# Sliding-window scores with 64-row matmuls against each group's own keys, in a two-layer hybrid decoder trunk

## The chip, the cores and the metric

The kernel runs on one NeuronCore of a Trainium2 chip, as one program. The metric is the device time of one execution in microseconds (us). The core has five engines that run side by side, each with its own queue of instructions in order: TensorE (matrix multiplies; the profile lists its multiplies as PE and its weight loads as PEld), VectorE (DVE), ScalarE (ACT), GpSimd (POOL) and SyncE (SP, which here issues most DMAs). They wait for one another through semaphores. Matmuls read from SBUF, the on-chip memory of 128 partitions, and write to PSUM, the accumulators, which are divided into banks of 512 fp32 values per partition.

## What is computed

The reference is a trunk of two layers over 256 tokens of width 1024. Each layer has a half-step SwiGLU, a layer norm, three token mixers side by side on the same normalised stream (gated DeltaNet, sliding-window attention with sinks, attention over a memory), gates that merge them, an output projection, a layer norm, and a second half-step SwiGLU with a layer norm. The change touches the sliding-window attention alone:

```python
SWA_HEADS = 8; SWA_KV_HEADS = 2; SWA_DH = 64; WINDOW = 128; SEQ = 256

def sliding_window_attention(q, k, v, sinks):
    Hkv, G, dh, W = SWA_KV_HEADS, SWA_HEADS // SWA_KV_HEADS, SWA_DH, WINDOW
    nb = S_ // W
    qb = q.reshape(B_, nb, W, Hkv, G, dh)
    kb, vb = band(k), band(v)          # the block before and the block itself
    s = jnp.einsum('bnqhgd,bnkhd->bnhgqk', qb, kb) * (dh ** -0.5)
    s = jnp.where(mask, s, NEG_INF)    # 0 <= t - key < W
    m = jnp.maximum(s.max(-1, keepdims=True), sink)
    p = jnp.exp(s - m)
    p = p / (p.sum(-1, keepdims=True) + jnp.exp(sink - m))
    o = jnp.einsum('bnhgqk,bnkhd->bnqhgd', p, vb)
```

Eight query heads of 64 features share two groups of keys and values, four heads each. The 256 tokens make two blocks of 128; the first block sees 128 keys, its own, the second sees 256.

## The kernel before

**Numbers.** Most products are made from pairs: an fp32 value is split into a high part in the type fp32r and a low part, also fp32r, that holds what the high part leaves over (`split`, line 115: a ScalarE cast, then a VectorE subtraction). A product is three matmuls, high by high, high by low and low by high (`mm3`, line 131). A matmul in fp32r is one record in the trace, one in plain fp32 is two.

**Weights.** All weights come as one stream, in units of 128 partitions by 1024 columns (`unit`, line 99): a DMA on SP's queue into `raw`, the cast to `whi` on ScalarE, the subtraction to `wlo` on VectorE. The consumers take them in stream order.

**Order.** Inside `mixers` (line 460) the order of TensorE's work is fixed by hand: every matmul and transpose goes through `pe` (line 121), which keeps program order while `pinned` is set. Steps of the sliding attention, the memory attention and the DeltaNet recurrence are placed between groups of projection matmuls by `weave` (line 137): a generator yields after each group, and the functions listed under that number run next. On the other engines instructions keep the order in which a scheduler places them.

**Sliding attention.** The projection of the keys is one bank with 128 features by 256 tokens: features 0 to 63 belong to key group 0, features 64 to 127 to group 1 (line 760). Lines 761 to 763 split it into `swk`, a high and a low tile of 128 partitions by 2 groups by 256 tokens. In slot `v` only the 64 partitions of group `v` are written; the other 64 were set to zero once, at the start of the program, by two ScalarE copies (lines 92 to 94). The queries (`sq_`, line 660) are laid out so that one tile of 128 partitions holds a head of group 0 in its upper half and a head of group 1 in its lower half. `sq_` index `2 * hh + j` picks such a pair.

`w_scores(tb, hh)` (line 665) makes the scores of token block `tb` for the four heads of `hh`. One `mm3` per pair takes the 128x128 query tile as weights and moves both slots of the zero-padded keys, 2 x `nk` columns, where `nk` is 128 at `tb` 0 and 256 at `tb` 1: the zeros keep the groups apart. At `tb` 0 both pairs fit into one PSUM bank, at `tb` 1 each takes a bank of its own. The banks come from `at()` (line 65), a pool of two that the transposes and values of both attentions share. A VectorE instruction (line 677) scales each bank, adds the mask and writes `pp`. The softmax follows: the row maximum, the sinks, exponentials on ScalarE, the reciprocal, the scaling (lines 678 to 692). `w_turn` transposes the probabilities, `w_values` multiplies them with the values.

In the order of work (lines 939 to 958) `w_scores(0, 0)` and `w_scores(0, 1)` stand after steps 7 and 8 of the first gates projection, `w_scores(1, 0)` after step 4 of the first branch projection, `w_scores(1, 1)` after step 2 of the second gates projection. `w_values(0)` comes one step after `w_scores(1, 0)`. All of it happens once in each layer.

Of the kernel before, what the change touches and what calls it, by code (L numbers as in the profile page):

```python
# [11 lines left out]
F32R = mybir.dt.float32r  # L12
I32 = mybir.dt.int32
AF = mybir.ActivationFunctionType
ALU = mybir.AluOpType
AX = mybir.AxisListType

P = 128
D = 1024
S = 256  # L20
# [18 lines left out]
def tile_trunk(ctx, tc, x, xT, mem, wst, lnp, memln, cvw, rows, cst, out):  # L39
    nc = tc.nc  # L40
    pc = ctx.enter_context(tc.tile_pool(name="pc", bufs=1))
# [16 lines left out]
    def T(pool, shape, tag, dt=F32, bufs=None):  # L58
        kw = {} if bufs is None else {"bufs": bufs}
        return pool.tile(shape, dt, tag=tag, name=nm(tag), **kw)  # L60
# [4 lines left out]
    def at():  # L65
        return T(psT, [P, 512], "at")
# [22 lines left out]
    nea = pc.tile([P, NL, 4], F32, name="nea")  # L89
    zero = pc.tile([P, 1], F32, name="zero")  # L90
    nc.gpsimd.memset(zero, 0.0)
    swk = [pc.tile([P, 2, S], F32R, name=f"swk{i}") for i in range(2)]
    for t in swk:
        nc.scalar.copy(t.rearrange("p v k -> p (v k)"), zero.to_broadcast([P, 2 * S]))


    pos = [0]
# [17 lines left out]
    def split(hi, lo, src):  # L115
        nc.scalar.copy(hi, src)  # L116
        return nc.vector.tensor_tensor(lo, src, hi.bitcast(F32), op=ALU.subtract).ins  # L117
# [3 lines left out]
    def pe(ins):  # L121

        return tc.keep_in_program_order(ins) if pinned[0] else ins

    def matmul(*a, **k):
        return pe(nc.tensor.matmul(*a, **k))  # L126
# [4 lines left out]
    def mm3(o, l, r, first, last, skip=False):  # L131
        (lh, ll), (rh, rl) = l, r
        matmul(o, lh, rh, start=first, stop=False, skip_group_check=skip)
        matmul(o, lh, rl, start=False, stop=False, skip_group_check=skip)
        matmul(o, ll, rh, start=False, stop=last, skip_group_check=skip)

    def weave(work, steps):

        for n, _ in enumerate(work, 1):
            for f in steps.get(n, ()):  # L140
                f()

    def projB(xt, nt, kpu, behind=None):
        g = projB_parts(xt, nt, kpu, behind)
        while True:
            try:
                next(g)
            except StopIteration as e:
                return e.value
# [37 lines left out]
    def halves(xt, use):  # L187

        for i in range(2):
            (b,) = yield from projB_parts(xt, 2, 4)  # L190
            use(i, b)
# [256 lines left out]
    def memory_kv(mT, behind):  # L448
        mx = (lambda k: mT[k // 4][:, k % 4, :], lambda k: mT[2 + k // 4][:, k % 4, :])
        mkT = (T(pu, [P, 4, S], "u10", F32R), T(pu, [P, 4, S], "u7", F32R))  # L450
        for i, b in enumerate(projB(mx, 4, 2)):
            split(*(t[:, 2 * i:2 * i + 2, :] for t in mkT), b)
        mv_ = T(pu, [P, 2, 512], "u11")
        outs = [[acc()] for _ in range(2)]
        projA(mx, 512, 2, KD, outs, behind=behind, held=range(4))
        for tb in range(2):
            nc.scalar.copy(mv_[:, tb, :], outs[tb][0])
        return mkT, mv_

    def mixers(l, hT, mkT, mv_, post):  # L460
# [8 lines left out]
        for tb in range(2):  # L469
            a, b = outs[tb]  # L470
# [70 lines left out]
        def col(tag):  # L541
            return T(pu, sh, tag)
# [11 lines left out]
        t = col("spt")  # L554
# [105 lines left out]
        sq_ = (T(pu, [P, 4, S], "u5", F32R), T(pu, [P, 4, S], "sql", F32R))  # L660
# [4 lines left out]
        def w_scores(tb, hh):  # L665

            ts = slice(tb * P, (tb + 1) * P)
            nk = P if tb == 0 else 2 * P
            msk = cs[:, C_SW + P:C_SW + 2 * P] if tb == 0 else cs[:, C_SW:C_SW + 2 * P]
            pr = wpr[tb, hh] = T(p2, [P, 4, S], "pp")  # L670
            for j in range(0, 2, 2 * P // nk):

                nj = 2 * P // nk
                ps = at().rearrange("p (j v k) -> p j v k", j=nj, v=2)
                for i in range(nj):
                    mm3(ps[:, i], [t[:, 2 * hh + j + i, ts] for t in sq_], [t[:, :, 0:nk] for t in swk], True, True)
                nc.vector.scalar_tensor_tensor(pr[:, 2 * j:2 * j + 2 * nj, :nk], ps.rearrange("p j v k -> p (j v) k"), 0.125, msk.unsqueeze(1).to_broadcast([P, 2 * nj, nk]), op0=ALU.mult, op1=ALU.add)
            mxs = T(p3, [P, 2, 2], "mx")
            sums = T(p3, [P, 4], "sums")
            sk = T(p3, [P, 2, 2], "sk")  # L680
            sink = sinks[:, 2 * hh:2 * hh + 2, :]
            flat = lambda t: t.rearrange("p i v -> p (i v)")
            nc.vector.tensor_reduce(flat(mxs), pr[:, :, :nk], axis=AX.X, op=ALU.max)
            nc.vector.tensor_tensor(mxs, mxs, sink, op=ALU.max)
            nc.vector.tensor_tensor(sk, sink, mxs, op=ALU.subtract)
            nc.scalar.activation(flat(sk), flat(sk), AF.Exp)
            nc.vector.tensor_scalar(flat(mxs), flat(mxs), -1.0, None, ALU.mult)
            for h in range(4):
                nc.scalar.activation(pr[:, h, :nk], pr[:, h, :nk], AF.Exp, bias=mxs[:, h // 2, h % 2:h % 2 + 1], accum_out=sums[:, h:h + 1])
            nc.vector.tensor_tensor(sums, sums, flat(sk), op=ALU.add)  # L690
            wpr["end"] = nc.vector.reciprocal(sums, sums).ins
            [nc.scalar.mul(pr[:, h, :nk], pr[:, h, :nk], sums[:, h:h + 1]) for h in range(4)]
# [65 lines left out]

        weave(halves(xt, use_xq), {3: [tok_v]})
        (b,) = projB(xt, 1, 8)  # L760
        for kv in range(2):
            hs = slice(kv * 64, kv * 64 + 64)
            split(swk[0][hs, kv, :], swk[1][hs, kv, :], b[hs, 0, :])
        weave(halves(xt, use_sq), {
            1: [decay],
            2: [lambda: spread(0), lambda: x_scores(0)],
# [153 lines left out]
        def branch(n, o):  # L920
# [22 lines left out]
            5: [lambda: x_turn(1)],  # L943
            6: [lambda: x_values(1)],
            7: [lambda: w_scores(0, 0)],
            8: [lambda: w_scores(0, 1)]})
        weave(branch(0, oX), {
            2: [lambda: w_turn(0, 0)],
            3: [lambda: w_turn(0, 1), begin_inverse],
            4: [lambda: w_scores(1, 0)]})  # L950
        weave(gates(1), {
            1: [lambda: w_values(0), double],
# [59 lines left out]
    for l in range(NL):  # L1012
        mT = []
        mid = memory_T(mT, l)
        if l == 0:
            mid.update({5: small, 7: lambda: xres(0), 9: lambda: xres(1)})
        post = Post(lnp[l, 0, 0], lnp[l, 0, 1])
        f1.rest(hT, 4, [((pu, "u12"), (pu, "u13")), ((p2, "gt"), (p2, "gt"))], post, mid, ends)
        kv = memory_kv(mT, post.end)
        if l == 0:  # L1020
            nc.scalar.activation(nea, rw[:, :, 8:12], AF.Exp)
            nc.vector.tensor_scalar(nea, nea, -1.0, None, ALU.mult)
        post2 = Post(lnp[l, 1, 0], lnp[l, 1, 1])
        mixers(l, post.hT, *kv, post2)
        f2 = Ffn()
        begin(f2, post2.hT)
        last = l == NL - 1
        post = Post(lnp[l, 2, 0], lnp[l, 2, 1], last)
        f2.rest(post2.hT, 6, [((pu, a), (pu, b)) for a, b in (("w0", "w1"), ("w2", "w3"), ("u11", "u12"))] + [((pu, "u13"), (p2, "pp"))], post, behind=post2.end)
        ends = post.end  # L1030
        if not last:
            f1, hT = Ffn(), post.hT
            begin(f1, hT)
# [86 lines left out]
```

## Time and profile before

| | |
|---|---|
| median of 3 runs | 1296.47 us (1295.87 to 1298.31) |
| profiled execution, its own time | 1298.02 us |
| its span, first to last instruction | 1296.2 us |
| mean granted TensorE clock | 0.998 |
| instructions | 20444 |
| DMA | 240.25 MB, mean 185 GB/s |

The profile is of one execution. Its views: a summary of busy times by engine; groups of instructions by line, engine, operation, tiles and shape, with their count; one tile's instructions; a timeline, in which neighbouring equal instructions are merged into a row with a count; windows, with the busy time of each engine in a stretch; and the chain of work that ended last, followed back from the last instruction to whatever released each step. A timeline row gives the start, the length of the merged stretch, the engine, the line, the operation, output and inputs by tile name, the rows and columns of the array that are used (128\*128), the shape that is moved, the count, and in brackets the idle time before it with what ended it. Lines 126 and 129 are helpers through which all matmuls and transposes of the mixers go, so the tile names tell them apart: `at<-swk,u` and `at<-swk,sql` are the scores with the high and the low part of the queries. Matmuls are pipelined: each record lasts longer than the step to the next one.

### The profile page before, as it was taken

How to read it: one execution, taken by the hardware profiler on the slowest of the kernel's cores; microseconds unless marked ns; L12 is line 12 of the kernel's file. 1: busy time of each engine (PE TensorE's matmuls, PEld its weight loads, DVE VectorE, ACT ScalarE, POOL GpSimd, SP SyncE). 2: the span in 40 equal slices, each digit the busy share in tenths (PEclk: the TensorE clock that was granted, in tenths of full speed). 3: DMA queues.
4: the chain of work that ended last, by engine and by line, in shares of the span. 5: the costliest groups of instructions: out<-in, count | busy, mean ns of one | idle time of the engine just before them, and what ended most of it. 6: DMA issues, size and time to landing. Idle time of an engine off the chain costs nothing.

```text
span 1296.2 us, 20444 instructions
## 1 busy us (share of the span) xinstructions
PE 1277.9 (99%) x7832; PEld 1116.2 (86%) x7832; DVE 888.4 (69%) x1430; ACT 708.5 (55%) x1177; POOL 77.2 (6%) x135
## 2 busy tenths in 40 slices
PE   8999999999999999999999999999999999999997
PEld 6888889999878888888888888899988788888886
DVE  6787556796647777665677674759867388777645
ACT  6656444666674546554455654456656654565541
POOL 0000000102311000000000000000033100000000
PEclk9999999999999999999999999999999999999999
DMA  7867564654533636555665555556453256455553
GB/s 266 276 210 244 193 229 128 220 174 135 161 131 130 228 129 211 191 185 192 228 222 200 188 186 192 199 175 201 163 165 131 98 182 224 149 194 194 189 189 111
DMA packets 68577, 240.25 MB, mean 185 GB/s; under 512 B 8160, under 2 KB 9312, under 8 KB 68480
## 3 DMA queue, kind: packets, MB, share of 16 engines
q1 hardware_dynamic: 66176, 232.53, 53.1%
q0 software_dynamic: 2304, 6.43, 1.8%
q8 instruction: 61, 1.00, 0.3%
q14 instruction: 36, 0.29, 0.1%
HBM read 235.64 MB, written 3.28 MB: 184 GB/s over the span
## 4 chain that ended last, share of the span: by engine, by line
PE 89%; DVE 4%; DMA 4%; ACT 2%; issue 1%; SPq 0%; DVEq 0%; ACTq 0%
PE acc L126 78%; PE at L126 4%; DMA raw<-in_wst_dram 3%; PE sm L126 3%; PE sm L129 1%; ACT whi L116 1%; DVE wlo L117 1%; PE acc L340 1%; PE acc L337 1%; DMA pp<-in_mem_dram 1%; PE acc L338 1%; PE at L129 1%; DVE bnst L282 0%; DVE u L117 0%; DVE h L301 0%
## 5 line engine op out<-in xcount | busy, mean ns | idle before, releaser
L117 DVE TENSOR_TENSOR wlo<-raw,whi 128x1024 fp32r<-128x1024 f32 (+2 forms) x403 | 487.4, 1214 | 308.7 <-ACT whi L116 307.2
L116 ACT CAST whi<-raw 128x1024 fp32r<-128x1024 f32 (+2 forms) x403 | 414.4, 1033 | 366.7 <-DMA raw<-in_wst_dram 99.0
L126 PE MATMUL acc<-hT,whi 128*128 128x512 f32 (+1 forms) x1952 | 524.9, 357 | 0.0
L126 PEld LDWEIGHTS acc<-hT,wlo 128*128 128x128 f32 x1616 | 304.6, 189 | 56.0
L126 PE MATMUL acc<-hT,wlo 128*128 128x256 f32 x1616 | 347.6, 279 | 0.0
L126 PEld LDWEIGHTS acc<-hT,whi 128*128 128x128 f32 x1952 | 299.8, 190 | 0.2
L126 PE MATMUL acc<-whi,u 128*128 128x512 f32 (+1 forms) x800 | 246.7, 373 | 0.0
L126 PEld LDWEIGHTS acc<-whi,u 128*128 128x128 f32 x800 | 150.1, 188 | 27.7 <-DVE t L184 1.2
L126 PE MATMUL acc<-whi,hT 128*128 128x512 f32 (+1 forms) x544 | 168.4, 380 | 5.6 <-ACT whi L116 5.6
L126 PE MATMUL acc<-wlo,u 128*128 128x512 f32 (+1 forms) x400 | 148.4, 371 | 0.0
L126 PEld LDWEIGHTS acc<-whi,hT 128*128 128x128 f32 x544 | 100.6, 189 | 23.7 <-ACT whi L116 5.6
L126 PE MATMUL acc<-wlo,hT 128*128 128x512 f32 (+1 forms) x272 | 101.9, 375 | 0.0
L126 PEld LDWEIGHTS acc<-wlo,u 128*128 128x128 f32 x400 | 75.5, 189 | 12.2
L372 ACT ACTIVATE t<-t 128x256 f32<-128x256 f32 x80 | 33.4, 417 | 60.4 <-DVE t L184 59.9
L184 DVE TENSOR_TENSOR t<-t,acc 128x256 f32<-128x256 f32 x160 | 59.9, 415 | 0.0
L126 PEld LDWEIGHTS acc<-wlo,hT 128*128 128x128 f32 x272 | 51.5, 190 | 8.2 <-DVE wlo L117 0.9
L183 ACT COPY t<-acc 128x256 f32<-128x256 f32 x160 | 51.5, 369 | 0.1
L116 ACT CAST u<-t 128x256 fp32r<-128x256 f32 x80 | 32.1, 401 | 20.4 <-DVE t L374 20.4
L374 DVE TENSOR_TENSOR t<-t 128x256 f32<-128x256 f32 x80 | 33.9, 424 | 9.2 <-ACT t L372 7.7
L126 PE MATMUL at<-whi,u 128*128 128x256 f32 x152 | 39.0, 283 | 0.0
L117 DVE TENSOR_TENSOR u<-t,u 128x256 fp32r<-128x256 f32 x80 | 33.6, 420 | 7.1 <-ACT u L116 7.1
L489 DVE SCALAR_TENSOR_TENSOR t<-acc,cw,t 128x255 f32<-128x255 f32 (+2 forms) x72 | 34.5, 479 | 0.9
(248 smaller groups left out, 1250.4 us busy)
## 6 DMA issues: line engine op xcount, KB each, us to landing
raw<-in_wst_dram SPq DMA_DIRECT2D x409, 512.0 KB, 3.6
raw<-in_wst_dram SPq DMA_DIRECT2D x16, 324.0 KB, 3.0
gB<-in_lnp_dram SPq DMA_DIRECT2D x6, 512.0 KB, 6.4
bB<-in_lnp_dram SPq DMA_DIRECT2D x6, 512.0 KB, 5.9
mdr<-w POOLq DMA_DIRECT2D x4, 512.0 KB, 6.8
w<-dr POOLq DMA_DIRECT2D x4, 512.0 KB, 8.8
w<-mdr POOLq DMA_DIRECT2D x4, 512.0 KB, 5.2
t<-in_xT_dram SPq DMA_DIRECT2D x4, 256.0 KB, 5.3
```

The lines of the kernel that those rows point to most:

```text
L116: nc.scalar.copy(hi, src)
L117: return nc.vector.tensor_tensor(lo, src, hi.bitcast(F32), op=ALU.subtract).ins
L126: return pe(nc.tensor.matmul(*a, **k))
L129: return pe(nc.tensor.transpose(*a))
L183: nc.scalar.copy(y[:, t], banks[t][:, S:])
L184: nc.vector.tensor_tensor(y[:, t], y[:, t], banks[t][:, 0:S], op=ALU.add)
L337: nc.tensor.matmul(ps, hT[0][:, k, ts], hi[:, c], start=k == 0, stop=False)
L338: nc.tensor.matmul(ps, hT[0][:, k, ts], lo[:, c], start=False, stop=False)
L340: nc.tensor.matmul(ps, hT[1][:, k, ts], hi[:, c], start=False, stop=k == KD - 1)
L372: nc.scalar.activation(y[:, 0], y[:, 0], AF.Silu)
L374: nc.vector.tensor_tensor(hf, y[:, 0], hf, op=ALU.mult)
L489: nc.vector.scalar_tensor_tensor(yc[:, j, d:], b[:, j, :S - d], w[:, t:t + 1], yc[:, j, d:], op0=ALU.mult, op1=ALU.add)
```

## The change

The keys lose their padding: `swk` is 128 partitions by 256 tokens, written by one `split`, and the clearing copies at the start go. `w_scores` asks for two banks at once, one for each key group. It issues, for each of the two pairs `j` and each of the three high and low combinations, two matmuls of 64 rows: the upper 64 partitions of query and keys into the first bank, the lower 64 into the second. At `tb` 0 a bank then holds 2 x 128 columns, at `tb` 1 2 x 256. Two evictions follow at either `tb`, one for each bank, which write every second head of `pp`. The values that are summed are the same but for the zeros.

```diff
-    swk = [pc.tile([P, 2, S], F32R, name=f"swk{i}") for i in range(2)]
-    for t in swk:
-        nc.scalar.copy(t.rearrange("p v k -> p (v k)"), zero.to_broadcast([P, 2 * S]))
+    swk = [pc.tile([P, S], F32R, name=f"swk{i}") for i in range(2)]
...
             pr = wpr[tb, hh] = T(p2, [P, 4, S], "pp")
-            for j in range(0, 2, 2 * P // nk):
-
-                nj = 2 * P // nk
-                ps = at().rearrange("p (j v k) -> p j v k", j=nj, v=2)
-                for i in range(nj):
-                    mm3(ps[:, i], [t[:, 2 * hh + j + i, ts] for t in sq_], [t[:, :, 0:nk] for t in swk], True, True)
-                nc.vector.scalar_tensor_tensor(pr[:, 2 * j:2 * j + 2 * nj, :nk], ps.rearrange("p j v k -> p (j v) k"), 0.125, msk.unsqueeze(1).to_broadcast([P, 2 * nj, nk]), op0=ALU.mult, op1=ALU.add)
+            banks = [at()[:, 0:2 * nk].rearrange("p (j k) -> p j k", j=2) for _ in range(2)]
+            for j in range(2):
+                for a, b, first, last in ((0, 0, True, False), (0, 1, False, False), (1, 0, False, True)):
+                    for v in range(2):
+                        hs = slice(v * 64, v * 64 + 64)
+                        matmul(banks[v][:, j, :], sq_[a][hs, 2 * hh + j, ts], swk[b][hs, 0:nk], start=first, stop=last, skip_group_check=True)
+            for v in range(2):
+                nc.vector.scalar_tensor_tensor(pr.rearrange("p (j v) k -> p j v k", v=2)[:, :, v, :nk], banks[v], 0.125, msk.unsqueeze(1).to_broadcast([P, 2, nk]), op0=ALU.mult, op1=ALU.add)
...
         (b,) = projB(xt, 1, 8)
-        for kv in range(2):
-            hs = slice(kv * 64, kv * 64 + 64)
-            split(swk[0][hs, kv, :], swk[1][hs, kv, :], b[hs, 0, :])
+        split(swk[0], swk[1], b[:, 0, :])
```

## The prediction

> **What bounds the kernel now.** I read the summary of busy times, the chain of work that ended last, and the busy times by window around the sliding scores.
>
> ```profile
> PE 1277.9 (99%) x7832; PEld 1116.2 (86%) x7832; DVE 888.4 (69%) x1430; ACT 708.5 (55%) x1177; POOL 77.2 (6%) x135
> PE 89%; DVE 4%; DMA 4%; ACT 2%; issue 1%; SPq 0%; DVEq 0%; ACTq 0%
> 346.00:363.00 17.00, 17.00 (x189) 13.21 (x188) 13.98 (x21) 10.49 (x22) 0.54 (x2) 1.00 0.58 187
> ```
>
> TensorE is 89% of the chain. In the third row (window, its length, busy PE, PEld, DVE, ACT, POOL, granted clock, DMA share), where layer 0 has its later sliding scores, it is busy 17.00 of 17.00 us at clock 1.00. So what the change adds to or takes from TensorE's stream there moves the end by as much; DVE and ACT have time left. A busy PE is not a full PE, so I cost by start-to-start steps, not by durations.
>
> The instructions that touch the keys (count, ns min/median/max):
>
> ```profile
> L126 PE MATMUL at<-swk,u x32: 277/336/398, 331.2 to 997.7; 128*128 128x256 f32 x16, 128*128 128x512 f32 x16
> L126 PEld LDWEIGHTS at<-swk,sql x16: 187/188/188, 331.3 to 997.7; 128*128 128x128 f32 x16
> L116 ACT CAST swk<-acc x4: 363/365/367, 287.6 to 930.1; 64x256 fp32r<-64x256 f32 x4
> L117 DVE TENSOR_TENSOR swk<-acc,swk x4: 406/418/427, 288.8 to 930.5; 64x256 fp32r<-64x256 f32 x4
> ```
>
> 32 + 16 = 48 matmuls: eight calls of `w_scores` (two layers, two row blocks `tb`, two head pairs `hh`) of six each, 256 columns wide at `tb` 0 and 512 at `tb` 1. One call of each, on PE's timeline:
>
> ```profile
> 331.22 0.40 PE L126 MATMUL at<-swk,u 128*128 128x256 f32 x2
> 331.45 0.28 PE L126 MATMUL at<-swk,sql 128*128 128x256 f32 x1
> 331.57 0.40 PE L126 MATMUL at<-swk,u 128*128 128x256 f32 x2
> 331.81 0.28 PE L126 MATMUL at<-swk,sql 128*128 128x256 f32 x1
> 331.92 0.39 PE L126 MATMUL acc<-whi,hT 128*128 128x512 f32 x1
> ...
> 347.27 0.62 PE L126 MATMUL at<-swk,u 128*128 128x512 f32 x2
> 347.73 0.39 PE L126 MATMUL at<-swk,sql 128*128 128x512 f32 x1
> 347.96 0.63 PE L126 MATMUL at<-swk,u 128*128 128x512 f32 x2
> 348.43 0.40 PE L126 MATMUL at<-swk,sql 128*128 128x512 f32 x1
> 348.66 0.40 PE L126 MATMUL acc<-whi,hT 128*128 128x512 f32 x1
> ```
>
> From first start to the next group's start a `tb` 0 call takes 331.92 - 331.22 = 0.70 us (0.12 a matmul), a `tb` 1 call 348.66 - 347.27 = 1.39 us (0.23 a matmul). All eight together: 4 x (0.70 + 1.39) = 8.4 us, so the change can win no more than a part of 0.65% of the time.
>
> **The change, part by part.** *Matmuls.* Each call now issues 12 matmuls of 64 rows, six for the upper half of the partitions and six for the lower, in turn, of 128 columns (`tb` 0) or 256 (`tb` 1). Were two halves to run at once, a call is six pairs; were they to take turns, twelve steps. The trace has no matmul of 64 rows by 128 columns; its nearest are smaller tiles of the array:
>
> ```profile
> 361.06 1.51 PE L126 MATMUL sm<-w,w 32*32 32x32 f32 x64
> L126 PE MATMUL sm<-w,w 32*32 32x32 f32 x224 | 6.2, 194 | 0.0
> 383.25 0.39 PE L126 MATMUL acc<-whi,hT 128*128 128x512 f32 x1
> 383.56 1.14 PE L126 MATMUL sm<-w,u 64*64 64x64 f32 x16
> 384.64 0.50 PE L126 MATMUL acc<-whi,u 128*128 128x512 f32 x1
> 384.98 0.39 PE L126 MATMUL acc<-wlo,u 128*128 128x512 f32 x1
> L126 PE MATMUL sm<-w,u 64*64 64x64 f32 x32 | 2.3, 222 | 0.0
> 351.51 1.08 PE L126 MATMUL at<-pt,swv 128*64 128x512 f32 x4
> 351.51 0.20 PEld L126 LDWEIGHTS at<-pt,swv 128*64 128x64 f32 x4 [0.35 <-DVE pp L677]
> 326.70 1.95 PE L126 MATMUL at<-pt,u 128*128 128x128 f32 x16
> L126 PE MATMUL at<-pt,u 128*128 128x128 f32 x64 | 7.8, 275 | 0.0
> 289.28 0.53 PEld L126 LDWEIGHTS sm<-g,cs 128*128 128x128 f32 x4
> ```
>
> Tiles at different places do run together. A full fp32 record of 128 columns steps at (1.95 - 0.275)/15 = 0.112 us, so one of 512 columns costs some 0.45 and the four of `w_values` some 1.8 in turn; they end in 1.08, and their four weight loads lie within 0.20 us. The 32x32 tiles step at (1.51 - 0.194)/63 = 0.021 us, the 64x64 ones at (1.14 - 0.222)/15 = 0.061, more than twice. But these tiles differ in columns; two halves of the rows with the same 128 columns are not shown. I take overlap, and keep twelve steps as the upper end.
>
> Step of a pair: with 256 columns 0.12, as a full matmul of 256 columns. With 128 columns no fp32r row exists. Lower end half of 0.12, 0.06. But each matmul loads 128 columns of weights, and where only 8 columns are moved the loads still step at (0.53 - 0.19)/3 = 0.113 us (last row; 0.19 is one load). Upper end an fp32 product of 128 columns, two records, 0.224. I take 0.113, the load's own pace, for a pair.
>
> *Change of tile shape.* Around the 64x64 burst the stream loses time. In: 383.56 - 383.25 = 0.31 for a step of 0.23, so 0.08. Out: its last matmul starts at 383.56 + 1.14 - 0.222 = 384.48 and the next comes 0.16 later, 0.10 more than its step of 0.06; the one after follows at 0.34 in place of 0.23, 0.11, as its weights of 128 columns were not loaded ahead. I add the same 0.11 for the first load of the new shape, also 128 columns: 0.08 + 0.11 + 0.10 + 0.11 = 0.40 us a call. Lower end 0 (loads ahead across the change), upper 0.54: the stream empties both ways, 0.39 - 0.23 = 0.16 in and 0.28 - 0.12 = 0.16 out, plus the two loads.
>
> The last is what the Trainium skill says, "TensorEngine Tiling (Array Packing)", Key Properties: changing the tiling mode drains TensorE. The trace agrees that a change costs, but with 0.08 and 0.10 for the bare gaps it shows less than a drain; by the rule the sum below would be 8 x 0.14 = 1.1 us higher.
>
> Sum: `tb` 1 call 6 x 0.12 + 0.40 = 1.12 against 1.39, -0.27; `tb` 0 call 6 x 0.113 + 0.40 = 1.08 against 0.70, +0.38. Four of each: 4 x 0.11 = +0.4 us. At `tb` 0 there is nothing to win: the padding made a 256-column matmul just as long as a weight load.
>
> *Banks and evictions.* Both `at` banks are asked for at a call's first two matmuls, the second earlier than before.
>
> ```profile
> 329.36 0.68 DVE L117 TENSOR_TENSOR u<-at,u 128x512 fp32r<-128x512 f32 x1
> 332.12 0.69 DVE L677 SCALAR_TENSOR_TENSOR pp<-at,cs 128x512 f32<-128x512 f32 x1 [2.08 <-PE at L126]
> 338.38 1.28 ACT L692 ACTIVATE pp<-pp,sums 128x128 f32<-128x128 f32 x4 [0.32 <-DVE sums L691]
> 340.85 0.60 PE L129 MATMUL at<-cs,pp 128*128 128x128 f32 x4
> 344.70 0.59 ACT L701 COPY pt<-at 128x512 f32<-128x512 f32 x1 [1.30 <-PE at L129]
> 349.90 1.28 DVE L677 SCALAR_TENSOR_TENSOR pp<-at,cs 128x512 f32<-128x512 f32 x2
> 353.55 0.69 DVE L117 TENSOR_TENSOR u<-at,u 128x512 fp32r<-128x512 f32 x1
> L184 DVE TENSOR_TENSOR t<-t,acc 128x256 f32<-128x256 f32 x160 | 59.9, 415 | 0.0
> ```
>
> The banks' last readers end at 330.04 (call at 331.22) and 345.29 (call at 347.27): 1.2 and 2.0 us of cover. `w_values` at 351.51 reuses the first bank, read out from 349.90 as before, since the wide evictions keep their size and DVE is behind work of its own there. Its own bank is read until 353.55 + 0.69 = 354.24, and the next call comes a whole `weave` step after it. At `tb` 0 one eviction of 0.69 becomes two of 256 columns, 2 x 0.415 = 0.83: 0.14 us more, twice a layer, on DVE. Behind it in DVE's queue stand a `wlo` split and the row maximum; the scaled probabilities are ready at 338.38 + 1.28 = 339.66, the transposes start at 340.85, 1.2 us later. Zero; without that cover 4 x 0.14 = 0.6 us.
>
> *Keys and zeros.* Two 64-row splits become one of 128 rows: 0.37 us of ACT and 0.42 of DVE fewer a layer, while PE streams the next projection. Zero; uncovered, a gain of 0.8 a layer. The clearing copies at the start:
>
> ```profile
> 0.74 1.28 ACT L94 ACT_TABLE_LOAD   x1 [0.74 <-PEq L1109]
> 2.03 1.14 ACT L94 CAST swk<-zero 128x512 fp32r<-128x512 f32 x2
> 3.57 0.62 ACT L116 CAST hT<-t 128x512 fp32r<-128x512 f32 x1 [0.41 <-DMA t<-in_xT_dram]
> ```
>
> They end before the first input lands, which the cast at 3.57 awaits: zero. The table load moves ahead of that cast; it waits for no data and should still run at the start. Were it to stand behind the wait, 1.28 us late.
>
> So +0.4 us: the profiled execution's own time, 1298.02 us (span 1296.2 and 1.8 around it; 1.55 above the median), becomes 1298.4, and the median of 1296.47 becomes **1296.9 us**. The gain at `tb` 1 and the loss at `tb` 0 nearly cancel.
>
> **Rivals.** *The halves take turns.* For it: no row shows two row halves with common columns together, and each needs its own load of 128 columns. Against: the 1.08 us of `w_values`. Place: the twelve matmuls of each call. 12 x 0.12 + 0.40 = 1.84 (+0.45) and 12 x 0.113 + 0.40 = 1.76 (+1.06): 4 x 1.51 = +6.0 us, 1302.5. With a mean of p us for a pair the sum is 4 x (12p + 0.80 - 2.09): zero at 0.11, and 2.5 us, about the 0.2% below, at 0.16; from there on this rival decides.
>
> *Narrow fp32r is slow.* At 128 columns a pair takes the fp32 product's 0.224: 6 x 0.224 + 0.40 = 1.74, +1.04 at `tb` 0; with -0.27 at `tb` 1, +3.1 us, 1299.6. For it: no fp32r row under 256 columns exists. Against: loads step at 0.113 whatever is moved. With turns as well: 12 x 0.224 + 0.40 = 3.09 (+2.39), and +0.45: +11.4 us, 1307.9.
>
> *The switch is cheap and loads overlap.* Pairs of 0.06 and 0.12, switching 0 to 0.20: 0.36 to 0.56 against 0.70 and 0.72 to 0.92 against 1.39, a gain of 2.4 to 4.0 us, 1292.4 to 1294.1. Against: both bursts of small tiles pay at entry and exit.
>
> **How the numbers follow.** Forecast 0.43 (its own range 1295 to 1299), turns 0.21, narrow 0.15, turns and narrow 0.05, cheap 0.16. A measurement of this kernel tells about 0.2%, 2.6 us. Faster: three quarters of cheap, 0.12. Slower: turns, both, two thirds of narrow, a little of the forecast: 0.21 + 0.05 + 0.10 + 0.03 = 0.39. The rest, 0.49, within. Range 1293.8 to 1303.0: it takes in narrow, most of turns and the upper end of cheap; the rest of these and both together stay out, some 0.15.
>
> **What would show it.** In the changed profile: a `tb` 1 call from its first start to the next group's start at 1.0 to 1.2 us (turns: 1.8; cheap: under 0.95); a `tb` 0 call at 1.0 to 1.2 (turns or narrow: over 1.6); the two halves' matmuls starting within some 0.02 us of each other; a matmul of the next projection 0.34 after the first. No wait of PE on the eviction of the scores beyond 0.1 us, and the first cast of `hT` still near 3.6. Calls as forecast and yet a time outside the forecast's own range would make the sum wrong: then a wait has opened elsewhere, first to be looked for where PE asks for weights split by DVE.

## The result

| | before | after |
|---|---|---|
| median, 11 runs each | 1297.99 us (1295.87 to 1299.32) | 1300.26 us (1298.40 to 1302.64) |
| profiled execution, its own time | 1298.02 us | 1300.88 us |
| its span | 1296.2 us | 1298.9 us |
| instructions | 20444 | 20539 |

The changed kernel takes 1.0019 times as long, with a 95% interval of 1.0011 to 1.0026: 2.3 us more, where the forecast was 0.4 more. The forecast of 1296.9 us started from 1296.47, the median of 3 runs of the kernel before; over 11 runs that median is 1297.99, so 1.5 us of the distance to 1300.26 belong to the base. The page of the changed kernel begins as the old one did, first the busy times, then the chain that ended last:

```profile
PE 1280.7 (99%) x7880; PEld 1115.3 (86%) x7880; DVE 885.6 (68%) x1432; ACT 707.1 (54%) x1173; POOL 77.9 (6%) x135
PE 86%; DVE 6%; DMA 5%; ACT 2%; issue 1%; SPq 0%; DVEq 0%; ACTq 0%
```

TensorE still sets the end. It has 48 more matmuls and 48 more loads; ScalarE's four instructions fewer and VectorE's two more are what the edit says. This view does not show where 2.3 us went.

**The calls.** PE's timeline of the changed kernel (start, length of the merged row, engine, line, operation), one call at `tb` 0, then one at `tb` 1, each with the matmul ahead of it and two behind. Line 124 is now the matmul helper.

```profile
332.10 0.39 PE L124 MATMUL acc<-whi,hT 128*128 128x512 f32 x1
332.42 0.44 PE L124 MATMUL at<-swk,u 64*128 64x128 f32 x4
332.70 0.27 PE L124 MATMUL at<-swk,sql 64*128 64x128 f32 x2
332.81 0.39 PE L124 MATMUL at<-swk,u 64*128 64x128 f32 x4
333.03 0.28 PE L124 MATMUL at<-swk,sql 64*128 64x128 f32 x2
333.24 0.50 PE L124 MATMUL acc<-whi,hT 128*128 128x512 f32 x1
333.57 0.39 PE L124 MATMUL acc<-wlo,hT 128*128 128x512 f32 x1
...
348.91 0.39 PE L124 MATMUL acc<-whi,u 128*128 128x512 f32 x1
349.23 0.50 PE L124 MATMUL at<-swk,u 64*128 64x256 f32 x4
349.57 0.28 PE L124 MATMUL at<-swk,sql 64*128 64x256 f32 x2
349.69 0.40 PE L124 MATMUL at<-swk,u 64*128 64x256 f32 x4
349.93 0.28 PE L124 MATMUL at<-swk,sql 64*128 64x256 f32 x2
350.13 0.50 PE L124 MATMUL acc<-whi,hT 128*128 128x512 f32 x1
350.47 0.40 PE L124 MATMUL acc<-wlo,hT 128*128 128x512 f32 x1
```

The reader is to see pairs. A row of x2 lasts 0.27 to 0.28 us, as long as one record of it: both halves run at the same time, and in the trace the second starts 0.003 to 0.004 us after the first. From the third pair on, a pair steps at (333.03 - 332.70)/3 = 0.11 us with 128 columns and (349.93 - 349.57)/3 = 0.12 with 256.

To compare a whole call fairly, I take it from the matmul ahead to the second behind, since the change of tile shape costs on both sides of it. `tb` 1: 350.47 - 348.91 = 1.56 us, before 0.23 + 1.39 + 0.23 = 1.85, so -0.29. `tb` 0: 333.57 - 332.10 = 1.47, before 0.23 + 0.70 + 0.23 = 1.16, so +0.31. Four of each nearly cancel.

**Where the time went.** The matmuls other than the scores are the same 7784 in both kernels and in the same order, so each can be set beside its counterpart; where the lag between them grows, time was lost. Within one layer's mixers the lag changes by more than 0.1 us at four places only (layer 0 / layer 1, us):

```
both calls at tb 0                                  +0.61 / +0.61
transposes of w_turn(0, 1)                          +0.16 / +0.27
both calls at tb 1                                  -0.58 / -0.56
a DeltaNet doubling step beside w_turn(1, 0)        +0.57 / +0.57
sum                                                 +0.76 / +0.89
```

That is 1.65 us, of which the eight calls are 0.08. The rest, 1.57, are matmuls that were not edited at all. Outside the mixers the lag rises from -0.53 to +1.65 us in the first 25 us, and later moves by up to 1.0 us in either direction, as at the layer norms.

The larger place is the doubling step. ScalarE's timeline there, after and then before; line 793 (796 before) copies a doubled matrix out of PSUM, line 700 (701) copies transposed probabilities, line 114 (116) is the cast of a weight unit:

```profile
373.05 0.81 ACT L793 COPY w<-sm 32x128 f32<-32x128 f32 x3
374.19 1.04 ACT L114 CAST whi<-raw 128x1024 fp32r<-128x1024 f32 x1 [0.34 <-PE acc L124]
375.26 0.26 ACT L793 COPY w<-sm 32x128 f32<-32x128 f32 x1
```

```profile
371.62 1.08 ACT L796 COPY w<-sm 32x128 f32<-32x128 f32 x4
372.73 0.58 ACT L701 COPY pt<-at 128x512 f32<-128x512 f32 x1
373.21 1.05 ACT L116 CAST whi<-raw 128x1024 fp32r<-128x1024 f32 x1
374.15 0.59 ACT L701 COPY pt<-at 128x512 f32<-128x512 f32 x1
```

The order of the queue has changed. Before, four copies run in a row; after, the weight cast stands between the third and the fourth. The cast waits 0.34 us for TensorE and then runs 1.04, and the fourth copy starts at 375.26, as the cast ends (374.19 + 1.04 = 375.23). TensorE, after and then before, at the same step:

```profile
374.09 0.59 PE L124 MATMUL sm<-w,w 32*32 32x32 f32 x16
375.57 0.59 PE L124 MATMUL sm<-w,w 32*32 32x32 f32 x16 [0.90 <-ACT w L793]
376.19 1.14 PE L127 MATMUL at<-cs,pp 128*128 128x128 f32 x8
377.09 0.48 PE L124 MATMUL acc<-whi,hT 128*128 128x512 f32 x1
```

```profile
372.79 0.89 PE L126 MATMUL sm<-w,w 32*32 32x32 f32 x32
373.61 0.66 PE L129 MATMUL at<-cs,pp 128*128 128x128 f32 x4
374.80 0.66 PE L129 MATMUL at<-cs,pp 128*128 128x128 f32 x4 [0.53 <-ACT pt L701]
375.21 0.48 PE L126 MATMUL acc<-whi,hT 128*128 128x512 f32 x1
```

The burst of 32 is cut in two by a wait of 0.90 us. The old order had a wait of its own here, 0.53, where the same cast stands between the two copies of `pt` (372.73 and 374.15). From the burst to the next projection it is 377.09 - 374.09 = 3.00 against 375.21 - 372.79 = 2.42: 0.58 lost a layer.

The smaller place starts in VectorE's and ScalarE's queues. VectorE in the changed kernel, first the evictions of `w_scores(0, 0)`, then those of `w_scores(0, 1)`, and behind them the old one's row of `w_scores(0, 1)`:

```profile
333.61 1.28 DVE L115 TENSOR_TENSOR wlo<-raw,whi 128x1024 fp32r<-128x1024 f32 x1 [2.50 <-ACT whi L114]
334.81 0.74 DVE L676 SCALAR_TENSOR_TENSOR pp<-at,cs 128x256 f32<-128x256 f32 x2
339.28 1.23 DVE L115 TENSOR_TENSOR wlo<-raw,whi 128x1024 fp32r<-128x1024 f32 x1 [2.27 <-ACT whi L114]
340.58 0.41 DVE L676 SCALAR_TENSOR_TENSOR pp<-at,cs 128x256 f32<-128x256 f32 x1
341.00 0.39 DVE L676 SCALAR_TENSOR_TENSOR pp<-at,cs 128x256 f32<-128x256 f32 x1
```

```profile
335.58 0.69 DVE L677 SCALAR_TENSOR_TENSOR pp<-at,cs 128x512 f32<-128x512 f32 x1 [0.28 <-PE at L126]
336.19 1.22 DVE L117 TENSOR_TENSOR wlo<-raw,whi 128x1024 fp32r<-128x1024 f32 x1
```

Before, both evictions (line 677; the first at 332.12, in the prediction) ran ahead of a weight subtraction. After, both pairs (line 676) stand behind one, although the data of the first are complete some 0.3 us before its subtraction starts, and those of the second some 3.5 us before the first of its evictions. A pair of evictions takes 0.74 us, near the 0.83 forecast; what matters is that the softmax starts later. At the end of the second softmax are ScalarE's scaling of the probabilities and the transposes of `w_turn(0, 1)`, after and then before:

```profile
344.90 1.28 ACT L691 ACTIVATE pp<-pp,sums 128x128 f32<-128x128 f32 x4 [0.50 <-DVE sums L690]
345.79 0.77 PE L127 MATMUL at<-cs,pp 128*128 128x128 f32 x4
346.32 0.48 PE L124 MATMUL acc<-whi,u 128*128 128x512 f32 x1
```

```profile
342.12 1.28 ACT L692 ACTIVATE pp<-pp,sums 128x128 f32<-128x128 f32 x4
344.06 0.60 PE L129 MATMUL at<-cs,pp 128*128 128x128 f32 x4
344.42 0.48 PE L126 MATMUL acc<-whi,u 128*128 128x512 f32 x1
```

Before, the probabilities were ready at 343.40, 0.66 us ahead of the transposes; after, at 346.18, when the transposes have begun. From the first transpose to the next projection matmul it is 0.53 us against 0.36: 0.17.

### The profile page after: what moved, and what is told of

The parts are those of the page before. It is cut to its first block, busy times and chain, and to the rows that moved or that the text cites. A ratio compares the mean times of both kernels' runs of the same rounds, so it can differ in the third digit from the quotient of the medians.

```text
span 1298.9 us, 20539 instructions
## 1 busy us (share of the span) xinstructions
PE 1280.7 (99%) x7880; PEld 1115.3 (86%) x7880; DVE 885.6 (68%) x1432; ACT 707.1 (54%) x1173; POOL 77.9 (6%) x135
## 4 chain that ended last, share of the span: by engine, by line
PE 86%; DVE 6%; DMA 5%; ACT 2%; issue 1%; SPq 0%; DVEq 0%; ACTq 0%
PE acc L124 75%; DMA raw<-in_wst_dram 5%; PE at L124 4%; PE sm L124 3%; DVE wlo L115 1%; PE sm L127 1%; ACT whi L114 1%; PE acc L338 1%; PE at L127 1%; DVE h L298 1%; DVE bnst L280 1%; DVE h L395 1%; DVE u L115 1%; PE acc L335 1%; PE acc L336 1%
```

## The experiments

The theory: the matmuls cost what was forecast, and the loss comes from the places that ScalarE's and VectorE's instructions now have in their queues; a later start of the program was held to be part of it at first. The rivals: the start alone; the halves in truth taking turns somewhere; the new banks or the missing zeros. Each kernel was timed beside the kernel before on the same chip. The columns of the table are the four places of above, layer 0 / layer 1, each against the old kernel's one trace. In layer 0 of tb0 and serial, 0.1 us of the late transposes are those of `w_turn(0, 0)`.

| run | calls tb 0 | late transposes | calls tb 1 | doubling | median us | ratio to before (95%) |
|---|---|---|---|---|---|---|
| after | +0.61 / +0.61 | +0.16 / +0.27 | -0.58 / -0.56 | +0.57 / +0.57 | 1300.26 | 1.0019 (1.0011 to 1.0026) |
| clear | +0.61 / +0.61 | +0.27 / +0.26 | -0.56 / -0.56 | +0.57 / +0.57 | 1300.66 | 1.0025 (1.0017 to 1.0034) |
| tb0 | +0.61 / +0.61 | +0.70 / +0.14 | 0 / 0 | 0 / 0 | 1300.81 | 1.0019 (1.0010 to 1.0027) |
| tb1 | 0 / 0 | 0 / 0 | -0.54 / -0.47 | +0.59 / +0.55 | 1298.47 | 1.0008 (0.9998 to 1.0017) |
| cpA | +0.61 / +0.61 | +0.41 / +0.14 | -0.56 / -0.58 | +0.28 / +0.28 | 1299.74 | 1.0017 (1.0007 to 1.0027) |
| serial | +1.17 / +1.17 | +0.27 / 0 | +0.07 / +0.09 | +0.29 / +0.28 | 1301.70 | 1.0032 (1.0020 to 1.0045) |
| ordpt | +0.61 / +0.61 | +0.11 / 0 | -0.58 / -0.56 | -0.74 / -0.74 | 1297.48 | 0.9994 (0.9985 to 1.0003) |
| tb1pt | 0 / 0 | 0 / 0 | -0.56 / -0.56 | -0.74 / -0.74 | 1295.73 | 0.9982 (0.9973 to 0.9991) |
| beforept | 0 / 0 | 0 / 0 | 0 / 0 | -0.74 / -0.74 | 1295.61 | 0.9985 (0.9976 to 0.9994) |

### clear: the padded tiles and their zeros back

The 64-row matmuls stay, and read their keys out of the old padded tile.

```diff
+    swk = [pc.tile([P, 2, S], F32R, name=f"swk{i}") for i in range(2)]
+    for t in swk:
+        nc.scalar.copy(t.rearrange("p v k -> p (v k)"), zero.to_broadcast([P, 2 * S]))
...
-    matmul(banks[v][:, j, :], sq_[a][hs, 2 * hh + j, ts], swk[b][hs, 0:nk], ...)
+    matmul(banks[v][:, j, :], sq_[a][hs, 2 * hh + j, ts], swk[b][hs, v, 0:nk], ...)
...
-        split(swk[0], swk[1], b[:, 0, :])
+        for kv in range(2):
+            hs = slice(kv * 64, kv * 64 + 64)
+            split(swk[0][hs, kv, :], swk[1][hs, kv, :], b[hs, 0, :])
```

> The changed kernel with the padded keys, their clearing copies and the two 64-row splits kept; only the scores are 64-row matmuls, each reading its own slot. Theory 1 (the matmuls cancel; what is lost is lost in the order of ScalarE's and VectorE's queues in the mixers, some 0.8 us a layer, and part of it at the start of the program, which the missing clearing copies rearrange): the start is that of the kernel before again, some 0.5 to 1 us comes back, +1.3 to +1.8 us over the kernel before (ratio 1.0010 to 1.0014). Rival (the start is noise, all 2.3 us are lost in the mixers): as the changed kernel, ratio 1.0018. Rival (the start is all of it): ratio 1.0000 to 1.0003.

It is no faster than the changed kernel, and the mixers lose at the same places by like amounts. Of the three expectations only the rival's 1.0018, all lost in the mixers, lies in its interval. Zeros and splits are out as causes, and with them the later start: in the one profiled execution the start did come back (at the thirteenth matmul the lag is +0.30 us, where the changed kernel has +0.55 after having begun 0.53 ahead), but the median did not. That part of the theory fell.

What differs at the start can be read from the steps of the first projection matmuls. After the first two they start 0.43 us apart, and later 0.23. In ordpt, which does not clear either, the first short step comes at 9.0 us, in the changed kernel at 11.6, though the profile's column of the granted clock reads 1.00 for both between 9 and 11 us. In the ten profiled executions it comes between 8.9 and 11.6 us. The two kernels have the same code here, so I put this down to the execution. The Trainium skill, "TensorE: Matmul & The Clock Gate", Part 1, has a rule that would fit: the window over which TensorE's activity is judged runs free, so the moment of full speed varies between runs. That it is the clock, no column here shows.

### tb0 and tb1: one half of the change alone

Each has the padded tiles and their zeros, the 64-row matmuls at one token block and the old call at the other (the diff is that of tb0; tb1 asks for `tb == 1`).

```diff
+            if tb == 0:
                 banks = [at()[:, 0:2 * nk].rearrange("p (j k) -> p j k", j=2) for _ in range(2)]
...
+            else:
+                for j in range(0, 2, 2 * P // nk):
+                    nj = 2 * P // nk
+                    ps = at().rearrange("p (j v k) -> p j v k", j=nj, v=2)
...
```

> 64-row matmuls at the first token block only, padded full ones at the second; clearing copies kept. Theory 1: four calls at +0.30 us each, and the second transposes of the block late by 0.2 us a layer: +1.6 us, ratio 1.0012; no wait of TensorE for a ScalarE copy in the doubling. Rival (the narrow matmuls alone carry the loss): +2.3 us, ratio 1.0018. Rival (the loss sits at the second block): ratio 1.0002 or less.

> 64-row matmuls at the second token block only, padded full ones at the first; clearing copies kept. Theory 1: four calls at -0.29 us each, and in each layer some +0.6 us where TensorE waits 0.9 us in the doubling for a ScalarE copy that a weight cast was put ahead of: 0.0 us, ratio 1.0000. Rival (the order of the queues costs nothing in the end): -1.2 us, ratio 0.9991.

The calls add up as the prediction's sum wants: what `tb` 0 loses in one kernel, `tb` 1 wins in the other. The waits go with them. The late transposes come with the `tb` 0 half, and are worse by themselves (+0.70 in layer 0); that kernel lost 2.5 us (0.0019 x 1297.76), of which the four places make 2.06. Its time is the one that the rival gave, narrow matmuls alone; the rows say otherwise, as the calls are 1.22 of it and the transposes 0.84. The doubling's wait comes with the `tb` 1 half, and there eats its gain: -0.54 and +0.59. The interval of tb1 takes in the theory's 1.0000 and leaves out the rival's 0.9991. Neither kernel changes a line of the doubling step. The profile of tb1 lists a mean granted clock of 0.948 where the others have 0.998 or 0.999; its 512-column matmuls step at 0.23 us all the same.

### cpA: one edge of order

The changed kernel, with one weight cast told to stand behind the last doubling copy. `unit` already takes an instruction to stay behind.

```diff
-                nc.scalar.copy(M[o, :, e], ps[o])
+                hold["cp"] = nc.scalar.copy(M[o, :, e], ps[o]).ins
...
-            us = [unit() for _ in range(4)]
+            us = [unit(behind=hold.get("cp") if n == 1 and i == 2 else None) for i in range(4)]
```

> The changed kernel whole, with one edge of order added: the weight cast of the third unit of the second branch projection goes behind the last copy of the third doubling step on ScalarE. Nothing else moves. Theory 1: the wait of 0.9 us in each layer is gone, -1.2 us against the changed kernel, +1.1 us over the kernel before (ratio 1.0008). Rival (the wait is covered or comes back at the next step): as the changed kernel, ratio 1.0018.

Only half of it came. ScalarE's rows behind the four copies, and TensorE's row at that place:

```profile
375.63 1.04 ACT L114 CAST whi<-raw 128x1024 fp32r<-128x1024 f32 x1
376.70 1.07 ACT L701 COPY pt<-at 128x512 f32<-128x512 f32 x2
```

```profile
377.34 1.15 PE L127 MATMUL at<-cs,pp 128*128 128x128 f32 x8 [0.92 <-ACT pt L701]
```

The cast moved past the copies of the doubling and stands ahead of those of `pt`, so the next reader of the banks waits 0.92 us instead. The wait had not gone; the next instruction behind the cast had it. The doubling's place improves from +0.57 to +0.28 a layer, and the time cannot be told from the changed kernel's: 1.0017 is the rival's number, and the rows show its second form, a wait that comes back at the next step.

### ordpt: the changed kernel, with both queues in order

The cast now goes behind the `pt` copies, and two weight subtractions behind the evictions of the `tb` 0 scores; every matmul is the changed kernel's.

```diff
-                nc.vector.scalar_tensor_tensor(pr.rearrange(...)[:, :, v, :nk], banks[v], 0.125, ...)
+                ev = nc.vector.scalar_tensor_tensor(pr.rearrange(...)[:, :, v, :nk], banks[v], 0.125, ...)
+                hold[tb, hh] = ev.ins
...
-                nc.scalar.copy(wpT[tb][kb][...], ps.rearrange("p (i v) q -> p i v q", v=2))
+                hold["pt", tb, hh] = nc.scalar.copy(wpT[tb][kb][...], ps.rearrange("p (i v) q -> p i v q", v=2)).ins
...
-                    hi, lo = unit()
+                    hi, lo = unit(behind=hold.get((0, 1)) if n == 1 and j == 0 and uu == 0 else None)
...
-            us = [unit() for _ in range(4)]
+            us = [unit(behind=hold.get((0, 0)) if n == 0 and i == 3 else hold.get(("pt", 1, 0)) if n == 1 and i == 2 else None) for i in range(4)]
```

> The changed kernel whole with three edges of order: the evictions of the first block's scores ahead of the weight subtractions that had moved in front of them, and the same cast behind the transposed probabilities' copies. Theory 1: in the mixers the matmuls' sum is left (about 0 a layer), the late transposes (0.16 to 0.27 a layer) and the waits of 0.9 us are gone, and with them the 0.53 a layer of the kernel before: -0.9 us in the mixers, ratio 0.9993 to 1.0003 with the start of the program. Rival (the order was not the cause): as the changed kernel, ratio 1.0018.

By the ratios it is 3.2 us faster than the changed kernel (1.0019 to 0.9994), by the medians 2.8; by the four places it should be 2.94. The calls are untouched in the trace, +0.61 and -0.58 in layer 0; the late transposes shrink to +0.11 and 0, and the doubling goes below the old kernel's. Its ScalarE, then TensorE, at the doubling:

```profile
373.04 1.08 ACT L795 COPY w<-sm 32x128 f32<-32x128 f32 x4
374.14 1.07 ACT L702 COPY pt<-at 128x512 f32<-128x512 f32 x2
375.10 1.06 ACT L114 CAST whi<-raw 128x1024 fp32r<-128x1024 f32 x1
```

```profile
374.11 0.89 PE L124 MATMUL sm<-w,w 32*32 32x32 f32 x32
...
375.78 0.48 PE L124 MATMUL acc<-whi,hT 128*128 128x512 f32 x1
```

Copies first, the cast last, and no wait: 375.78 - 374.11 = 1.67 us, against 3.00 after and 2.42 before. So order alone is worth 1.33 us a layer at this one place. This is the test on which the explanation rests.

For the smaller place it is a weak test. In both layers the evictions of both calls now stand ahead of the subtractions, yet in layer 0 the scaling of the second softmax starts no earlier:

```profile
344.92 1.28 ACT L693 ACTIVATE pp<-pp,sums 128x128 f32<-128x128 f32 x4 [0.79 <-DVE sums L692]
```

The changed kernel has it at 344.90. ScalarE's queue has moved as well: a weight cast (336.35 to 337.40) now runs ahead of the first exponentials, which start at 337.41. Of the 0.43 us the edges took back 0.32, nearly all in layer 1; which of the two queues it was is not separated.

### tb1pt and beforept: what would beat both

tb1pt is the `tb` 1 half with the cast behind the `pt` copies; beforept is the old kernel with that edge and nothing else.

```diff
+                hold["pt", tb, hh] = nc.scalar.copy(wpT[tb][kb][...], ps.rearrange("p (i v) q -> p i v q", v=2)).ins
...
+            us = [unit(behind=hold.get(("pt", 1, 0)) if n == 1 and i == 2 else None) for i in range(4)]
```

> 64-row matmuls at the second token block only, clearing copies kept, and one edge of order: the weight cast of the third unit of the second branch projection goes behind the copies of the transposed probabilities. Theory 1: -0.56 us a layer from the matmuls as in the trace of the second block alone, and the wait of 0.53 us that the kernel before has in the same place is gone in both layers: -2.2 us, ratio 0.9983. Rival (the later cast makes TensorE wait for weights instead): ratio 0.9995 or more.

> The kernel before with the same edge of order alone. Theory 1: its two waits of 0.53 us are gone, -1.1 us, ratio 0.9992, and the kernel with the second block changed as well is another 1.1 us faster. Rival (the later cast is waited for): ratio 1.0000 or more.

Both beat both kernels, by about 2 us against the one before; for beforept that is more than the 1.1 expected. The edge gave -0.74 a layer in the old kernel, more than the wait of 0.53 that its profile named: the old transposes came in two rows that start 374.80 - 373.61 = 1.19 us apart, where in beforept all eight run as one row of 1.09. In the traces tb1pt has another -0.56 a layer from its calls, 1.1 us in all, and its span is 1.3 us shorter; the medians, 1295.73 and 1295.61, do not show it, and the intervals overlap: the 1.1 us expected over beforept did not come. Whether 64-row matmuls at `tb` 1 are worth having in time stays open.

beforept and ordpt have the same cast pinned (ordpt two subtractions as well), so set side by side they price the change on an order that no longer moves at the doubling. By the four places ordpt is 0.19 us slower, by its span 0.6, by the ratios 1.2 and by the medians 1.9; the two intervals overlap. Pinning brought the changed kernel 2.94 us by the places and the old one 1.48, so 1.46 of the loss was order. That nothing else is lost is not shown: in all eight kernels with 64-row matmuls the median lies further above that of the kernel before than the four places add up to, by 0.4 to 1.2 us, and in beforept it lies 0.8 lower.

### serial: all six upper matmuls ahead of the six lower

```diff
-            for j in range(2):
-                for a, b, first, last in (...):
-                    for v in range(2):
-                        hs = slice(v * 64, v * 64 + 64)
+            for v in range(2):
+                hs = slice(v * 64, v * 64 + 64)
+                for j in range(2):
+                    for a, b, first, last in (...):
```

> The changed kernel with the twelve matmuls of a call in another order: six of the upper half, then six of the lower. If TensorE overlaps two halves only where they stand next to each other, the halves take turns: 12 x 0.116 + 0.40 = 1.79 us a call of the second block in place of 1.10, 12 x 0.108 + 0.34 = 1.64 in place of 0.99 of the first, together +5.4 us over the changed kernel, ratio 1.0060. If it reaches past the six to the other half: as the changed kernel, ratio 1.0018.

It fell between, at 1.0032. PE's timeline of one `tb` 1 call:

```profile
350.05 0.50 PE L124 MATMUL at<-swk,u 64*128 64x256 f32 x2
350.39 0.28 PE L124 MATMUL at<-swk,sql 64*128 64x256 f32 x1
350.40 0.51 PE L124 MATMUL at<-swk,u 64*128 64x256 f32 x4
350.74 0.29 PE L124 MATMUL at<-swk,sql 64*128 64x256 f32 x2
350.86 0.40 PE L124 MATMUL at<-swk,u 64*128 64x256 f32 x2
351.10 0.28 PE L124 MATMUL at<-swk,sql 64*128 64x256 f32 x1
351.30 0.50 PE L124 MATMUL acc<-whi,hT 128*128 128x512 f32 x1
```

Rows of one half alone, then four and two matmuls of both, then one half alone again: nine steps, neither six nor twelve. The trace does not name the halves; a new one is told by its start 0.007 us after the third matmul, out of the step of 0.12. In all eight calls it starts there, with three upper ones that the kernel's order puts ahead of it still to come. The calls of a layer take (1.17 + 0.07) - (0.61 - 0.58) = 1.21 us more than in the changed kernel, 0.30 a call. So it matters that the halves are issued in turn; in the changed kernel this gives the full overlap.

## Why the prediction was near, and where it was wrong

**The time.** The measured 1300.26 lies in the range, but outside the forecast's own 1295 to 1299, and that the range took it in is in part luck: it was drawn wide for rivals that the rows rule out. By its time alone the change looks most like one of them, narrow fp32r with +3.1 us. Calls as forecast and a time beyond the forecast's own range were the prediction's sign that a wait has opened elsewhere, and so it was.

**Matmuls: right.** Halves run together, and a pair steps at 0.11 and 0.12 us where 0.113 and 0.12 were taken. The rivals of turns, of narrow fp32r and of both fall by these rows.

**Change of shape: right in size.** In: 332.42 - 332.10 = 0.32 for a step of 0.23, so 0.09. First pair at `tb` 1: 349.57 - 349.23 = 0.34 for two pairs, 0.10 more than 2 x 0.12; at `tb` 0 0.28, 0.06 more. Out: 333.24 - 333.03 = 0.21, 0.10 more than a pair's step, and 350.13 - 349.93 = 0.20, 0.08 more. Behind: 333.57 - 333.24 = 0.33 and 350.47 - 350.13 = 0.34 for 0.23, so 0.10 and 0.11. Sums 0.35 and some 0.38 for the 0.40 taken. By the prediction's estimate an emptied stream would have cost 0.16 each way; the drain that the Trainium skill states ("TensorEngine Tiling (Array Packing)", Key Properties) is not what these gaps of 0.08 to 0.10 show, and in the calls the 1.1 us more by that rule did not come.

**The sign on a call was drawn over the wrong stretch.** The prediction wanted 1.0 to 1.2 us from first start to the next group's start. It is 350.13 - 349.23 = 0.90 at `tb` 1, which by those words would be the cheap rival, and 333.24 - 332.42 = 0.82 at `tb` 0. Two of its four terms, the gap ahead and the late load behind, lie outside that stretch; with them it is 1.10 and 1.01, as forecast.

**Matmul sum: near.** +0.03 to +0.05 a layer in the trace, 0.08 us in all, for +0.43 forecast.

**Keys and zeros: right.** The table load runs at 0.74 as before and the first cast of `hT` is at 3.68, near 3.6; clear shows no gain from either.

**"Banks and evictions ... Zero": this step failed.** Its cover of 1.2 us was read off the first `tb` 0 call alone, with the rows in the order of the old queues; the second call's was 0.66 in the same trace. That order is no property of the code that stays: in the changed kernel it came out otherwise. After the change the second call's softmax comes late enough for 0.16 to 0.27 us a layer. The price without cover, 0.6 us in all, was near the 0.43 measured, but by another way: not longer evictions, later ones. The 0.57 a layer at the doubling was in no term: nothing of the change is there. The last lines of the prediction named the kind of fault, a wait opened elsewhere, but looked for it where TensorE asks for weights. It opened where TensorE asks for copies that stand behind a weight's cast.

**What remains.** Forecast 0.43, of which 0.08 came; waits of 1.57 came on top: 1.65 us, inside the interval of 1.4 to 3.4 us that the ratio gives. The rest, 0.6 us to the median, was not traced to a place: outside the mixers the lag differs by a microsecond or two between profiled executions, in both directions. As every kernel with 64-row matmuls has such a rest, it may be a cost of the change and not scatter; no run settles it. Why the scheduler chose the new order was not tested either, only what that order costs.

## What to carry to other kernels

Before a sum over edited instructions is trusted, ask which queues have an order that is not written down: an edit there moves instructions that it does not touch, and the sum is then made against an order that no longer exists. Look in the old profile for the places where TensorE has no slack and an engine in front of it has a long instruction free to move (here a 1.04 us cast among copies of 0.26), pin these behind what TensorE waits for, and measure the edit on top of the pinned order, as ordpt against beforept does here. And move such an instruction past everything that TensorE waits for: past half of it, the wait only changes its name.

## What the runs showed of the hardware

- Two 64-row matmuls of different halves, columns in common, start 0.003 to 0.004 us apart and take no longer than one (0.27 to 0.28 us). The Trainium skill, "TensorE: Matmul & The Clock Gate", Part 3, gives about 4 ns for such tiles; the trace agrees.
- The same section of the Trainium skill has matmuls start strictly in program order. In serial, by the order that the kernel fixes, they do not: in all eight calls the first of the lower half starts 0.007 us after the third of the upper half, before the other three. What sets the three was not tested.
- With 128 columns moved, fp32r kept the pace of the weight loads, 0.11 us a pair, against 0.12 with 256, so halving the columns wins nothing. The loads of 128 columns of weights step at 0.113 where only 8 columns are moved; that they set the pace here too is an inference.
- The profile's granted clock does not tell the pace of the matmuls: at 1.00 they stepped at 0.43 us early in the changed kernel and at 0.23 later, and in tb1, at 0.948, at 0.23.
